# The last 512 columns of an encoder layer's second token tile: nine steps whole, seven in halves, and the mean taken off first

## The chip, the cores and the metric

One core of a Trainium2 chip. The metric is device time of one execution in microseconds (us); the kernel before takes 1071.27 us, the median of 3 runs (1070.38 to 1072.18).

## The reference

One layer of an encoder on 256 tokens of width 2048: adaLN modulation, windowed attention, LayerNorm, then a squared-ReLU MLP of width 8192 and a second LayerNorm. The change touches only the end:

```
y = sq_relu_mlp(hff, mlp_w1[i], mlp_b1[i], mlp_w2[i], mlp_b2[i])
x = layer_norm(DEEPNORM_ALPHA * x + (1.0 + g_f[:, None, :]) * y, ln_mlp_g[i], ln_mlp_b[i])

def layer_norm(x, g, b):
    mu = jnp.mean(xf, axis=-1, keepdims=True)
    var = jnp.mean(jnp.square(xf - mu), axis=-1, keepdims=True)
    y = (xf - mu) * lax.rsqrt(var + LN_EPS)
    return (y * g.astype(jnp.float32) + b.astype(jnp.float32)).astype(x.dtype)
```

## The kernel before

Tokens lie on the 128 partitions, in two tiles t = 0 and 1; the 2048 columns are four blocks c = 0 to 3 of 512. `xs` holds the residual stream, two blocks in each [128, 1024] buffer (a g in the profile), and `part(xs, t, c)` is one block of one token tile. The MLP runs in four blocks of 2048 hidden units; `us` holds the squared activations of a block, in high and low halves, and `ws` the second weight matrix, split in the same way. A product of 128 hidden units is a step of three matmuls (`mm3`, L552 to L555): high x high, high x low, low x high, each [128 x 128] x [128 x 512] in fp32r with its own weight load. Products accumulate in PSUM tiles `pa` (one bank each, five in turn).

A scheduler orders the instructions on each engine by the program's order, by priorities (`tc.high_priority`) and by what depends on what. Engines then run apart and wait on semaphores; VectorE, ScalarE and SP each take their instructions in their order.

The end of the program, from L1255 on, is the last block's c = 3. For each t, 16 steps (`ff_mm`, 48 matmuls) fill one bank. `add_gated` (L833) multiplies it by the gate g2 (L836), adds it to xs (L837) and takes bn_stats of 512 columns (L838). For t = 0 follow `norm_scalars` and two passes over each of the four blocks: minus mean, times g (L1295), then times rstd, plus b (L1296), and the store (L1280): odd c from SP's queue, even c from ScalarE's. While TensorE makes t = 1, VectorE does this; before it, `scaled` (L1284) multiplies blocks 0 to 2 of t = 1 by -0.5 g.

For t = 1 the kernel writes the normalisation as z x q + (b + nm x g), with z = -0.5 g x, q = -2 rstd and nm = 0.5 x mean x q. `last_scalars` (L1258 to L1273) makes q from a square root on ScalarE (L1263) and a Newton step on VectorE (L1265 to L1270), and nm (L1272). TensorE adds b and nm x g in PSUM for c = 1, 2, 3: an identity matmul of b ahead of time (L1304), then a matmul of g with a diagonal dg of nm, which ScalarE writes (L1309, L1317). These two are fp32 matmuls, which the profile shows as two passes each. For c = 0 VectorE makes w = g x nm + b (L1313). Block 3 is scaled by L1284 late, since its sum is just done. Four output passes z x q + (bank or w) end the program (L1318), c = 0, 1, 2, 3, each with its store.

Of the kernel before, what the change touches and what calls it, by code (L numbers as in the profile page):

```python
# [21 lines left out]
NT = S // 128  # L22
# [6 lines left out]
LN_EPS = 1e-5  # L29
# [30 lines left out]
def hybrid_kernel(ctx: ExitStack, tc: tile.TileContext, a, out: bass.AP):  # L60
    nc = tc.nc
    cst = ctx.enter_context(tc.tile_pool(name="cst", bufs=1))
    sml = ctx.enter_context(tc.tile_pool(name="sml", bufs=4))
# [5 lines left out]
    psa = ctx.enter_context(tc.tile_pool(name="psa", bufs=5, space=PSUM))  # L69
# [28 lines left out]
    ident = cst.tile([128, 128], F32, name="ident")  # L98
# [5 lines left out]
    eps = cst.tile([128, 1], F32, name="eps")  # L104
# [377 lines left out]
    for tok in LOADS.split():  # L482
        n = [int(v) for v in tok[1:].split(",")]
# [29 lines left out]
    for n, (kg, fq) in enumerate(W1A):  # L513
        left = [m.n - m.planned for m, _, _ in m_ff]
# [32 lines left out]
    acc, xts, held, xs = {}, {}, {}, [None] * 4  # L547

    def part(tiles, t, c):
        return tiles[c][:, t * 512:t * 512 + 512]  # L550

    def mm3(ps, xh, xl, wh, wl, start, stop):  # L552
        nc.tensor.matmul(ps, xh, wh, start=start, stop=False)  # L553
        nc.tensor.matmul(ps, xh, wl, start=False, stop=False)  # L554
        S.prev = nc.tensor.matmul(ps, xl, wh, start=False, stop=stop).ins  # L555
# [118 lines left out]
    for tok in STEPS.split():  # L674
        n = int(tok[1:])
# [154 lines left out]
            nc.scalar.copy(oh, po)  # L830
            return lambda: nc.vector.tensor_sub(ol, po, f32(oh))

    def add_gated(ps, t, c, gt, stats):  # L833
        tmp = sml.tile([128, 512], F32, name="tmp", tag="t2", bufs=4)
        z = part(xs, t, c)
        nc.vector.tensor_tensor(tmp, ps, gt(c), op=OP.mult)  # L836
        nc.vector.tensor_add(z, z, tmp)  # L837
        nc.vector.bn_stats(stats[t][:, c], z)  # L838
# [82 lines left out]
    for n in range(21):  # L921
# [136 lines left out]
    g2 = None  # L1058
    uacc = [g4() for _ in range(4)]
    us = []  # L1060
    opened = {}
    for n, (kg, fq) in enumerate(W1A):
# [3 lines left out]
        wh, wl = S.main()  # L1066
        for fp in range(2):
            if kg % 2 == 0:
                opened[fq, fp] = psa.tile([128, 512], F32, name="pa")
            ps = opened[fq, fp]  # L1070
            for fi in range(2):
                o = ps[:, fi * 256:fi * 256 + 256]
                for k in range(4):
                    w = (fp * 2 + fi) * 4 + k
# [12 lines left out]
            elif kg == 3:  # L1087
                nc.vector.tensor_add(av, av, ps)
                u = g4(F32R)
# [127 lines left out]
    for blk in range(BLK - 1):  # L1217
        if blk:
            us, pm = ff_mixed(blk)
# [23 lines left out]
    st = [sml.tile([128, 4, 6], F32, name=f"st{t}", bufs=2) for t in range(NT)]  # L1243
    mid = gather(pm)
    for f in mid[:2]:
        f()
# [8 lines left out]

    ws = [S.main() for _ in range(4)]

    def last_scalars(st):  # L1258

        mv = sml.tile([128, 2], F32, name="mv")  # L1260
        nc.vector.bn_aggr(mv, st)
# [3 lines left out]
        nc.vector.tensor_scalar_add(ve, mv[:, 1:2], LN_EPS)  # L1265
        r0 = sml.tile([128, 1], F32, name="r0")
        nc.vector.reciprocal(r0, sd)
        q = sml.tile([128, 1], F32, name="qq")
        nc.vector.scalar_tensor_tensor(q, r0, ve, r0, op0=OP.mult, op1=OP.mult)
        nc.vector.scalar_tensor_tensor(q, q, -3.0, r0, op0=OP.add, op1=OP.mult)  # L1270
        nm = sml.tile([128, 1], F32, name="nmr")
        nc.vector.scalar_tensor_tensor(nm, mv[:, 0:1], 0.5, q, op0=OP.mult, op1=OP.mult)  # L1272
        return q, nm  # L1273

    def affine(c):
        return (gb[n][c // 2][:, (c % 2) * 512:(c % 2) * 512 + 512] for n in range(2))

    def store(t, c, z):
        q = nc.sync if c % 2 else nc.scalar
        q.dma_start(out[t * 128:t * 128 + 128, c * 512:c * 512 + 512], z)  # L1280

    def scaled(t, c):
        z, (g, b) = part(xs, t, c), affine(c)
        nc.vector.scalar_tensor_tensor(z, z, -0.5, g, op0=OP.mult, op1=OP.mult)  # L1284

    for t in range(NT):
        ps = psa.tile([128, 512], F32, name="pa")
        for kg in range(4):
            ff_mm(ps, us, kg, t, ws[kg], kg == 0, kg == 3)
        if t == 0:  # L1290
            add_gated(ps, t, 3, g2, st)
            mv, rstd = norm_scalars(st[t])
            for c in (1, 0, 2, 3):
                z, (g, b) = part(xs, t, c), affine(c)
                nc.vector.scalar_tensor_tensor(z, z, mv[:, 0:1], g, op0=OP.subtract, op1=OP.mult)  # L1295
                nc.vector.scalar_tensor_tensor(z, z, rstd, b, op0=OP.mult, op1=OP.add)  # L1296
                store(t, c, z)
            for c in range(3):
                scaled(1, c)
    pw = {}  # L1300
    for c in (1, 2, 3):
        pw[c] = psa.tile([128, 512], F32, name="pa")
        g, b = affine(c)
        tc.keep_in_program_order(nc.tensor.matmul(pw[c], ident, b, start=True, stop=False))  # L1304
    with tc.high_priority(200):
        add_gated(ps, 1, 3, g2, st)
        rstd, nm = last_scalars(st[1])
        dg = sml.tile([128, 128], F32, name="dg", tag="t2", bufs=4)
        nc.scalar.activation(dg, ident, AF.Copy, scale=nm)  # L1309
    scaled(1, 3)  # L1310
    g, b = affine(0)
    w = sml.tile([128, 512], F32, name="w", tag="t2", bufs=4)
    nc.vector.scalar_tensor_tensor(w, g, nm, b, op0=OP.mult, op1=OP.add)  # L1313
    for c in range(4):
        z, (g, b) = part(xs, 1, c), affine(c)
        if c:
            nc.tensor.matmul(pw[c], dg, g, start=False, stop=True)  # L1317
        nc.vector.scalar_tensor_tensor(z, z, rstd, pw[c] if c else w, op0=OP.mult, op1=OP.add)  # L1318
        store(1, c, z)


# [91 lines left out]
```

## Time and profile before

| | |
|---|---|
| median of 3 runs | 1071.27 us |
| the profiled execution's own time | 1071.01 us |
| its span, first to last instruction | 1069.2 us |
| TensorE matmuls busy | 1051.6 us |
| VectorE busy | 938.8 us |
| mean granted TensorE clock | 0.999 |
| last matmul of the second tile's c = 3 starts | 1057.52 us |
| last output pass starts | 1065.07 us |

Times in the rows are us from the start of the span. A row of the timeline has the start, the duration (of the whole run of instructions where it ends in xN), the engine, the line, the operation, the names out<-in, and in brackets the idle time before it and what ended that. A row of a group of lines has the count, busy us, the mean ns of one, and the idle time before them. PE is TensorE, PEld its weight loads, DVE VectorE, ACT ScalarE; SPq and ACTq are instructions that start a DMA.

### The profile page before, as it was taken

How to read it: one execution, taken by the hardware profiler on the slowest of the kernel's cores; microseconds unless marked ns; L12 is line 12 of the kernel's file. 1: busy time of each engine (PE TensorE's matmuls, PEld its weight loads, DVE VectorE, ACT ScalarE, POOL GpSimd, SP SyncE). 2: the span in 40 equal slices, each digit the busy share in tenths (PEclk: the TensorE clock that was granted, in tenths of full speed). 3: DMA queues.
4: the chain of work that ended last, by engine and by line, in shares of the span. 5: the costliest groups of instructions: out<-in, count | busy, mean ns of one | idle time of the engine just before them, and what ended most of it. 6: DMA issues, size and time to landing. Idle time of an engine off the chain costs nothing.

```text
span 1069.2 us, 15967 instructions
## 1 busy us (share of the span) xinstructions
PE 1051.6 (98%) x6162; PEld 853.7 (80%) x6162; DVE 938.8 (88%) x1396; ACT 620.1 (58%) x978; POOL 27.5 (3%) x54
## 2 busy tenths in 40 slices
PE   8999999999999999999999999999999999999997
PEld 6677677666677799988888888788888888888885
DVE  4689999979999998987579999999899887999997
ACT  5333347776772737643367776447677536767640
POOL 1000000001000000000000000000000001000000
PEclk9999999999999999999999999999999999999999
DMA  9999997799965998698824644974564773465742
GB/s 383 424 424 425 427 427 289 284 388 337 394 252 197 349 361 303 247 333 314 296 91 186 236 180 175 388 280 155 200 235 165 281 286 138 160 232 201 264 166 78
DMA packets 43516, 292.72 MB, mean 274 GB/s; under 512 B 5152, under 2 KB 5280, under 8 KB 9648
## 3 DMA queue, kind: packets, MB, share of 16 engines
q1 hardware_dynamic: 39456, 279.85, 68.0%
q0 software_dynamic: 3232, 10.50, 3.0%
q10 hardware_dynamic: 752, 1.35, 0.4%
q8 instruction: 48, 0.79, 0.3%
q14 instruction: 28, 0.23, 0.1%
HBM read 289.57 MB, written 2.11 MB: 273 GB/s over the span
## 4 chain that ended last, share of the span: by engine, by line
PE 87%; DMA 6%; DVE 4%; ACT 1%; issue 1%; SPq 0%; ACTq 0%; DVEq 0%
PE pa L1108 16%; PE pa L553 14%; PE pa L555 14%; PE pa L554 14%; PE pa L1110 9%; DMA raw<-in_modm 4%; PE pm L361 3%; PE pa L1081 3%; PE pa L1082 3%; PE pa L1078 3%; DVE g L401 2%; PE pa L766 1%; PE pt L810 1%; PE pa L827 1%; DMA raw<-in_w 1%; PE pt L554 1%
## 5 line engine op out<-in xcount | busy, mean ns | idle before, releaser
L297 ACT CAST wh<-raw 128x1024 fp32r<-128x1024 f32 (+1 forms) x332 | 335.9, 1021 | 268.3 <-PE pa L555 150.9
L248 DVE TENSOR_TENSOR wl<-raw,wh 128x1024 fp32r<-128x1024 f32 (+1 forms) x332 | 388.0, 1183 | 61.9 <-ACT wh L297 57.3
L553 PE MATMUL pa<-wh,g 128*128 128x512 f32 x648 | 258.1, 399 | 3.6 <-ACT g L576 2.9
L554 PE MATMUL pa<-wl,g 128*128 128x512 f32 x648 | 253.4, 391 | 0.5 <-DVE wl L248 0.5
L555 PE MATMUL pa<-wh,g 128*128 128x512 f32 x648 | 252.9, 392 | 0.9 <-DVE g L578 0.9
L1108 PE MATMUL pa<-g,wh 128*128 128x512 f32 x768 | 191.5, 391 | 0.0
L1108 PEld LDWEIGHTS pa<-g,wh 128*128 128x128 f32 x768 | 140.5, 188 | 28.4 <-issue 0.8
L553 PEld LDWEIGHTS pa<-wh,g 128*128 128x128 f32 x648 | 121.6, 188 | 40.9 <-issue 6.8
L555 PEld LDWEIGHTS pa<-wh,g 128*128 128x128 f32 x648 | 121.5, 188 | 29.7 <-DVE g L578 3.0
L554 PEld LDWEIGHTS pa<-wl,g 128*128 128x128 f32 x648 | 121.8, 188 | 25.6 <-DVE wl L248 1.2
L1110 PEld LDWEIGHTS pa<-g,wl 128*128 128x128 f32 x768 | 104.8, 190 | 7.5
L1110 PE MATMUL pa<-g,wl 128*128 128x256 f32 x768 | 107.1, 282 | 0.0
L401 DVE SCALAR_TENSOR_TENSOR g<-raw,cact,g 128x1024 f32<-128x1024 f32 x66 | 84.0, 1280 | 2.7 <-DMA raw<-in_modf 1.6
L1081 PE MATMUL pa<-g,wh 128*128 128x256 f32 x256 | 72.9, 285 | 0.2 <-DVE g L1004 0.2
L1078 PE MATMUL pa<-g,wh 128*128 128x256 f32 x256 | 72.7, 285 | 0.4 <-ACT g L996 0.3
L1082 PE MATMUL pa<-g,wl 128*128 128x256 f32 x256 | 72.3, 283 | 0.0
L248 DVE TENSOR_TENSOR raw<-raw 128x1024 fp32r<-128x1024 f32 x48 | 58.4, 1222 | 0.6 <-ACT raw L297 0.6
L297 ACT CAST raw<-raw 128x1024 fp32r<-128x1024 f32 x48 | 49.8, 1044 | 4.9 <-DVE raw L259 3.6
L401 DVE SCALAR_TENSOR_TENSOR g4b<-raw,cact,g4b 128x1024 f32<-128x1024 f32 x32 | 40.2, 1283 | 13.8 <-DMA raw<-in_modgf 13.8
L1081 PEld LDWEIGHTS pa<-g,wh 128*128 128x128 f32 x256 | 49.1, 192 | 1.4 <-DVE g L1004 0.9
L1078 PEld LDWEIGHTS pa<-g,wh 128*128 128x128 f32 x256 | 49.0, 192 | 0.8 <-ACT g L996 0.8
L1082 PEld LDWEIGHTS pa<-g,wl 128*128 128x128 f32 x256 | 49.1, 192 | 0.0
(234 smaller groups left out, 1244.1 us busy)
## 6 DMA issues: line engine op xcount, KB each, us to landing
raw<-in_w1b SPq DMA_DIRECT2D x48, 1024.0 KB, 6.6
raw<-in_w SPq DMA_DIRECT2D x40, 1024.0 KB, 7.0
raw<-in_modm SPq DMA_DIRECT2D x32, 1024.0 KB, 11.4
raw<-in_modf SPq DMA_DIRECT2D x32, 1024.0 KB, 7.3
raw<-in_wqkv SPq DMA_DIRECT2D x24, 1024.0 KB, 12.5
raw<-in_w2s SPq DMA_DIRECT2D x24, 1024.0 KB, 4.8
raw<-in_modgm SPq DMA_DIRECT2D x16, 1024.0 KB, 7.2
raw<-in_wo SPq DMA_DIRECT2D x16, 1024.0 KB, 7.3
```

The source lines that it names most:

```text
L248: self.pinned(nc.vector.tensor_sub(l[:, :w], r, f32(self.hs[n])[:, :w]))
L297: self.pinned(nc.scalar.copy(h[:, :s.shape[-1]], s))
L361: i = nc.tensor.matmul(self.ps[32 * j:32 * j + 32, :w], lhsT[j] if type(lhsT) is list else lhsT, rhs[j], start=self.first, stop=stop)
L401: nc.vector.scalar_tensor_tensor(p[:, :e], s, cact[:, kt:kt + 1], p[:, :e], op0=OP.mult, op1=OP.add)
L553: nc.tensor.matmul(ps, xh, wh, start=start, stop=False)
L554: nc.tensor.matmul(ps, xh, wl, start=False, stop=False)
L555: S.prev = nc.tensor.matmul(ps, xl, wh, start=False, stop=stop).ins
L1078: x = nc.tensor.matmul(o, wh(w, 128), hh, start=new, stop=False)
L1081: nc.tensor.matmul(o, wh(w, 128), hl, start=False, stop=False)
L1082: nc.tensor.matmul(o, wl(w, 128), hh, start=False, stop=end)
L1108: nc.tensor.matmul(ps, wh(k, 128), ff_in(k), start=k == 0, stop=False)
L1110: nc.tensor.matmul(ps[:, :256], wl(k, 128), ff_in(k)[:, :256], start=False, stop=k == NK - 1)
```

## The change

Lines of the changed kernel differ from those of the one before by 1 to 16.

- The tile's 16 steps of t = 1 are now nine whole ones (LAST = 9) into one bank, seven of the left 256 columns into the same bank, and then seven of the right 256 columns into a second bank.
- `add_gated` takes a column range. It is called for the left half, for the right half of the first bank (no statistics, since the sum isn't complete), and then for the second bank, with its own bn_stats; the statistics of a tile have five groups.
- The normalisation of t = 1 is rearranged. TensorE's identity matmul puts z = -0.5 g x of blocks 1, 2, 0 into PSUM (L1326 of the changed kernel), and dm = 0.5 x mean x identity, written by VectorE straight after the aggregate (L1267), adds 0.5 x mean x g (L1333). Block 3 is done on VectorE: (z - mean) x gneg with gneg = -0.5 g (L1273, gneg made at L1305). The output passes are bank x q + b (L1334), in the order c = 3, 1, 2, 0. nm, dg and w go.
- `keep` holds `last_scalars` and the output passes in the order they are written in.

```
+LAST = 9
...
-    def add_gated(ps, t, c, gt, stats):
+    def add_gated(ps, t, c, gt, stats, cols=slice(0, 512), n=0):
         tmp = sml.tile([128, 512], F32, name="tmp", tag="t2", bufs=4)
-        z = part(xs, t, c)
-        nc.vector.tensor_tensor(tmp, ps, gt(c), op=OP.mult)
-        nc.vector.tensor_add(z, z, tmp)
-        nc.vector.bn_stats(stats[t][:, c], z)
+        z = part(xs, t, c)[:, cols]
+        nc.vector.tensor_tensor(tmp[:, cols], ps[:, cols], gt(c)[:, cols], op=OP.mult)
+        nc.vector.tensor_add(z, z, tmp[:, cols])
+        if stats:
+            nc.vector.bn_stats(stats[t][:, c + n], z)
...
+    keep = tc.keep_in_program_order
+    def last_scalars(st, g):
         mv = sml.tile([128, 2], F32, name="mv")
-        nc.vector.bn_aggr(mv, st)
+        keep(nc.vector.bn_aggr(mv, st))
+        dm = sml.tile([128, 128], F32, name="dm", tag="t2", bufs=4)
+        keep(nc.vector.tensor_scalar(dm, ident, mv[:, 0:1], 0.5, op0=OP.mult, op1=OP.mult))
         sd = sml.tile([128, 1], F32, name="sd")
-        nc.scalar.activation(sd, mv[:, 1:2], AF.Sqrt, bias=eps)
+        keep(nc.scalar.activation(sd, mv[:, 1:2], AF.Sqrt, bias=eps))
...
+        z = part(xs, 1, 3)
+        keep(nc.vector.scalar_tensor_tensor(z, z, mv[:, 0:1], g, op0=OP.subtract, op1=OP.mult))
...
-        nm = sml.tile([128, 1], F32, name="nmr")
-        nc.vector.scalar_tensor_tensor(nm, mv[:, 0:1], 0.5, q, op0=OP.mult, op1=OP.mult)
-        return q, nm
+        return q, dm
...
+    gneg = sml.tile([128, 512], F32, name="w", tag="t2", bufs=4)
+    nc.vector.tensor_scalar_mul(gneg, gb[0][1][:, 512:], -0.5)
+    ps, pr = (psa.tile([128, 512], F32, name="pa") for _ in range(2))
+    left, right = slice(0, 256), slice(256, 512)
+
+    def last(n, p, cols, start, stop):
+        s = slice((n % 2) * 256 + 128, (n % 2) * 256 + 256)
+        u, (wh, wl) = us[n // 2], ws[n // 4]
+        mm3(p[:, cols], u[:, :512][:, s], u[:, 512:][:, s], wh(n % 4)[:, cols], wl(n % 4)[:, cols], start, stop)
+
+    for n in range(LAST):
+        last(n, ps, slice(0, 512), n == 0, False)
+    for n in range(LAST, 16):
+        last(n, ps, left, False, n == 15)
+    with tc.high_priority(200):
+        add_gated(ps, 1, 3, g2, st, left)
+        add_gated(ps, 1, 3, g2, None, right)
+    for n in range(LAST, 16):
+        last(n, pr, right, n == LAST, n == 15)
     pw = {}
-    for c in (1, 2, 3):
+    for c in (1, 2, 0):
         pw[c] = psa.tile([128, 512], F32, name="pa")
-        g, b = affine(c)
-        tc.keep_in_program_order(nc.tensor.matmul(pw[c], ident, b, start=True, stop=False))
+        keep(nc.tensor.matmul(pw[c], ident, part(xs, 1, c), start=True, stop=False))
     with tc.high_priority(200):
-        add_gated(ps, 1, 3, g2, st)
-        rstd, nm = last_scalars(st[1])
-        dg = sml.tile([128, 128], F32, name="dg", tag="t2", bufs=4)
-        nc.scalar.activation(dg, ident, AF.Copy, scale=nm)
-    scaled(1, 3)
-    g, b = affine(0)
-    w = sml.tile([128, 512], F32, name="w", tag="t2", bufs=4)
-    nc.vector.scalar_tensor_tensor(w, g, nm, b, op0=OP.mult, op1=OP.add)
-    for c in range(4):
+        add_gated(pr, 1, 3, g2, st, right, 1)
+        rstd, dm = last_scalars(st[1], gneg)
+    for c in (3, 1, 2, 0):
         z, (g, b) = part(xs, 1, c), affine(c)
-        if c:
-            nc.tensor.matmul(pw[c], dg, g, start=False, stop=True)
-        nc.vector.scalar_tensor_tensor(z, z, rstd, pw[c] if c else w, op0=OP.mult, op1=OP.add)
+        if c < 3:
+            nc.tensor.matmul(pw[c], dm, g, start=False, stop=True)
+        keep(nc.vector.scalar_tensor_tensor(z, pw.get(c, z), rstd, b, op0=OP.mult, op1=OP.add))
         store(1, c, z)
```

The order on the engines differs only in this last stretch. On VectorE before, from the first tile's last output passes to the second tile's aggregate (g_2615 is block 3 of xs, pa the bank, st_9680 the statistics of t = 1):

```order
L1296 SCALAR_TENSOR_TENSOR g_2613<-g_2613,r_9923,g_9674 128x512
L1296 SCALAR_TENSOR_TENSOR g_2615<-g_2615,r_9923,g_9674 128x512
L836 TENSOR_TENSOR tmp<-pa,g4b 128x512
L837 TENSOR_TENSOR g_2615<-g_2615,tmp 128x512
L838 BN_STATS st_9680<-g_2615 128x6
L1261 BN_AGGR mv<-st_9680 128x2
```

and in the changed kernel:

```order
L1300 SCALAR_TENSOR_TENSOR g_2613<-g_2613,r_9923,g_9674 128x512
L837 TENSOR_TENSOR tmp<-pa,g4b 128x256 x2
L838 TENSOR_TENSOR g_2615<-g_2615,tmp 128x256 x2
L840 BN_STATS st_9680<-g_2615 128x6
L1300 SCALAR_TENSOR_TENSOR g_2615<-g_2615,r_9923,g_9674 128x512
L837 TENSOR_TENSOR tmp<-pa,g4b 128x256
L838 TENSOR_TENSOR g_2615<-g_2615,tmp 128x256
L840 BN_STATS st_9680<-g_2615 128x6
L1265 BN_AGGR mv<-st_9680 128x2
```

The early work on the first bank stands ahead of the first tile's fourth output pass, and that pass ahead of the last right half (the seven steps in the second bank). On VectorE from the aggregate to the end, before:

```order
L1284 SCALAR_TENSOR_TENSOR g_2615<-g_2615,g_9672 128x512
L1265 TENSOR_SCALAR ve<-mv 128x1
L1267 RECIPROCAL r_10009<-sd 128x1
L1269 SCALAR_TENSOR_TENSOR qq<-r_10009,ve 128x1
L1270 SCALAR_TENSOR_TENSOR qq<-qq,r_10009 128x1
L1272 SCALAR_TENSOR_TENSOR nmr<-mv,qq 128x1
L1313 SCALAR_TENSOR_TENSOR w<-g_9671,nmr,g_9673 128x512
L1318 SCALAR_TENSOR_TENSOR g_2609<-g_2609,qq,w 128x512
L1318 SCALAR_TENSOR_TENSOR g_2611<-g_2611,qq,pa 128x512
L1318 SCALAR_TENSOR_TENSOR g_2613<-g_2613,qq,pa 128x512
L1318 SCALAR_TENSOR_TENSOR g_2615<-g_2615,qq,pa 128x512
```

and in the changed kernel:

```order
L1267 TENSOR_SCALAR dm<-ident,mv 128x128
L1271 TENSOR_SCALAR ve<-mv 128x1
L1273 SCALAR_TENSOR_TENSOR g_2615<-g_2615,mv,w 128x512
L1275 RECIPROCAL r_10043<-sd 128x1
L1277 SCALAR_TENSOR_TENSOR qq<-r_10043,ve 128x1
L1278 SCALAR_TENSOR_TENSOR qq<-qq,r_10043 128x1
L1334 SCALAR_TENSOR_TENSOR g_2615<-g_2615,qq,g_9674 128x512
L1334 SCALAR_TENSOR_TENSOR g_2611<-pa,qq,g_9673 128x512
L1334 SCALAR_TENSOR_TENSOR g_2613<-pa,qq,g_9674 128x512
L1334 SCALAR_TENSOR_TENSOR g_2609<-pa,qq,g_9673 128x512
```

dm, on which TensorE waits, now stands first, and block 0's output, whose store goes from ScalarE's queue, last. Another row that moved: the scaling of g (w<-g_9672, L1305) stands in the changed kernel between L837 and L838 of the first tile's c = 3. On TensorE the 48 matmuls of t = 1 are followed by the identity products and those with dg or dm as before.

More of the change, by code (lines that the diff above doesn't have):

```diff
@@ L1242, in hybrid_kernel @@
             nc.gpsimd.dma_start(gb[n][h], a["lnrow"][2 + n:3 + n, h * 1024:h * 1024 + 1024].partition_broadcast(128))
-    st = [sml.tile([128, 4, 6], F32, name=f"st{t}", bufs=2) for t in range(NT)]
+    st = [sml.tile([128, 5, 6], F32, name=f"st{t}", bufs=2) for t in range(NT)]
     mid = gather(pm)
@@ L1256, in hybrid_kernel @@
     ws = [S.main() for _ in range(4)]
-    def last_scalars(st):
+    keep = tc.keep_in_program_order
+    def last_scalars(st, g):
         mv = sml.tile([128, 2], F32, name="mv")
-        nc.vector.bn_aggr(mv, st)
+        keep(nc.vector.bn_aggr(mv, st))
+        dm = sml.tile([128, 128], F32, name="dm", tag="t2", bufs=4)
+        keep(nc.vector.tensor_scalar(dm, ident, mv[:, 0:1], 0.5, op0=OP.mult, op1=OP.mult))
         sd = sml.tile([128, 1], F32, name="sd")
-        nc.scalar.activation(sd, mv[:, 1:2], AF.Sqrt, bias=eps)
+        keep(nc.scalar.activation(sd, mv[:, 1:2], AF.Sqrt, bias=eps))
         ve = sml.tile([128, 1], F32, name="ve")
-        nc.vector.tensor_scalar_add(ve, mv[:, 1:2], LN_EPS)
+        keep(nc.vector.tensor_scalar_add(ve, mv[:, 1:2], LN_EPS))
+        z = part(xs, 1, 3)
+        keep(nc.vector.scalar_tensor_tensor(z, z, mv[:, 0:1], g, op0=OP.subtract, op1=OP.mult))
         r0 = sml.tile([128, 1], F32, name="r0")
-        nc.vector.reciprocal(r0, sd)
+        keep(nc.vector.reciprocal(r0, sd))
         q = sml.tile([128, 1], F32, name="qq")
-        nc.vector.scalar_tensor_tensor(q, r0, ve, r0, op0=OP.mult, op1=OP.mult)
-        nc.vector.scalar_tensor_tensor(q, q, -3.0, r0, op0=OP.add, op1=OP.mult)
-        nm = sml.tile([128, 1], F32, name="nmr")
-        nc.vector.scalar_tensor_tensor(nm, mv[:, 0:1], 0.5, q, op0=OP.mult, op1=OP.mult)
-        return q, nm
+        keep(nc.vector.scalar_tensor_tensor(q, r0, ve, r0, op0=OP.mult, op1=OP.mult))
+        keep(nc.vector.scalar_tensor_tensor(q, q, -3.0, r0, op0=OP.add, op1=OP.mult))
+        return q, dm
     def affine(c):
@@ L1284, in scaled @@
         nc.vector.scalar_tensor_tensor(z, z, -0.5, g, op0=OP.mult, op1=OP.mult)
[L1286 to L1299, printed above, removed]
+    ps = psa.tile([128, 512], F32, name="pa")
@@ new lines, in hybrid_kernel @@
+    for kg in range(4):
+        ff_mm(ps, us, kg, 0, ws[kg], kg == 0, kg == 3)
+    add_gated(ps, 0, 3, g2, st)
+    mv, rstd = norm_scalars(st[0][:, :4])
+    for c in (1, 0, 2, 3):
+        z, (g, b) = part(xs, 0, c), affine(c)
+        nc.vector.scalar_tensor_tensor(z, z, mv[:, 0:1], g, op0=OP.subtract, op1=OP.mult)
+        nc.vector.scalar_tensor_tensor(z, z, rstd, b, op0=OP.mult, op1=OP.add)
+        store(0, c, z)
+    for c in range(3):
+        scaled(1, c)
+    gneg = sml.tile([128, 512], F32, name="w", tag="t2", bufs=4)
```

## The prediction

> **What bounds the kernel now.** The page's first part says which engine fills the span, the windows view then shows the last 22 us, which are all that the change touches.
>
> ```profile
> span 1069.2 us, 15967 instructions
> ...
> PE 1051.6 (98%) x6162; PEld 853.7 (80%) x6162; DVE 938.8 (88%) x1396; ACT 620.1 (58%) x978; POOL 27.5 (3%) x54
> ```
> ```profile
> core 0: us, PE busy (x) PEld busy (x) DVE busy (x) ACT busy (x) POOL busy (x), PEclk, DMA share, GB/s
> 1047.00:1058.00 11.00, 11.00 (x50) 9.06 (x49) 8.84 (x19) 0.20 (x1) 0.00 (x0) 1.00 0.23 88
> 1058.00:1069.20 11.20, 5.32 (x12) 1.81 (x10) 7.24 (x15) 0.69 (x2) 0.00 (x0) 0.92 0.26 101
> ```
>
> TensorE is busy 98% of the span. Up to 1058 it has no gap (11.00 of 11.00); after that comes a tail of 11.2 us in which it works 5.32 and VectorE 7.24. The profiled execution took 1071.01 us, 1.8 more than its span; the median of the runs shown is 0.26 above it. Everything before the second tile's column block c = 3 keeps its place, so the sum is over this tail. The chain that ended last gives its links:
>
> ```profile
> 1057.68 0.24 PE pa L555
> 1057.94 0.70 DVE tmp L836
> 1058.67 0.70 DVE g L837
> 1059.39 0.70 DVE st L838
> 1060.12 0.26 DVE mv L1261
> 1060.39 0.55 DVE g L1284
> 1061.10 0.23 DVE qq L1269
> 1061.74 0.41 ACT dg L1309
> 1062.19 2.86 PE pa L1317 x6
> 1065.07 0.75 DVE g L1318
> ```
>
> Three VectorE passes of 0.69 after the last product, the statistics, a scalar chain up to dg, then 2.86 us of TensorE (three fp32 products, two passes each) and the last output pass, ending at 1065.82. The remaining 3.39 us are the last store and the program's close.
>
> **Part 1, TensorE: 21 matmuls of 512 columns become 42 of 256.** From the timeline and from the line of the only short matmuls of this shape:
>
> ```profile
> 1048.00 0.39 PE L555 MATMUL pa<-wh,g 128*128 128x512 f32 x1
> ...
> 1057.52 0.39 PE L555 MATMUL pa<-g4b,g 128*128 128x512 f32 x1
> ```
> ```profile
> 1004.76 1.11 PE L1110 MATMUL pa<-g,wl 128*128 128x256 f32 x8
> ```
> ```profile
> L1110 PEld LDWEIGHTS pa<-g,wl x768: 187/192/192, 542.2 to 1005.5; 128*128 128x128 f32 x192
> L1110 PE MATMUL pa<-g,wl x768: 277/283/283, 542.4 to 1005.6; 128*128 128x256 f32 x192
> ```
>
> The first two rows are 42 steps apart (48 matmuls of the tile, five issued earlier between those of the first tile), so one 512-column matmul costs 9.52 / 42 = 0.227. Eight of 256 columns take 1.11, the last of them its own 0.28, so the step is 0.83 / 7 = 0.119; I take 0.12. The 21 that change began at 1057.52 - 20 x 0.227 = 1052.98. Now the last left matmul starts at 1052.98 + 20 x 0.12 = 1055.38 and ends 0.28 later, 1055.67; the last right one starts at 1057.90 and ends at 1058.19. So TensorE ends 0.28 later than before (1057.91), but the left half, and the right half of the first nine steps, are ready 2.2 us earlier. Bounds of the step: half of a whole one, 0.113, and the weight load's 0.192 if loads didn't overlap; I take 0.12 because the eight rows are the same shape.
>
> The Trainium skill (TensorE: Matmul & The Clock Gate, Back-to-back issue gap) tabulates 262 cycles for 256 columns and 518 for 512, at 2.4 GHz 109 and 216 ns. By that the cut would cost 21 x 2.5 ns = 0.05 us instead of 0.28, an estimate; the trace's 0.119 against 0.227 says more, and I go by the trace.
>
> **Part 2, VectorE up to the statistics.** Here lies the point: was VectorE free to use the early half? Its rows, then the groups that price the new shapes:
>
> ```profile
> 1045.70 1.89 DVE L1284 SCALAR_TENSOR_TENSOR g<-g,g 128x512 f32<-128x512 f32 x3
> 1048.20 0.69 DVE L836 TENSOR_TENSOR tmp<-pa,g4b 128x512 f32<-128x512 f32 x1 [0.61 <-PE pa L555]
> 1048.92 0.69 DVE L837 TENSOR_TENSOR g<-g,tmp 128x512 f32<-128x512 f32 x1
> ...
> 1053.83 2.74 DVE L1296 SCALAR_TENSOR_TENSOR g<-g,r,g 128x512 f32<-128x512 f32 x4
> 1057.94 0.69 DVE L836 TENSOR_TENSOR tmp<-pa,g4b 128x512 f32<-128x512 f32 x1 [1.37 <-PE pa L555]
> ```
> ```profile
> L1041 DVE TENSOR_TENSOR g<-uf,g 128x256 fp32r<-128x256 f32 x48 | 20.3, 422 | 3.7 <-ACT g L1040 3.7
> ...
> L1050 DVE TENSOR_TENSOR sf<-uf 128x128 f32<-128x128 f32 x24 | 7.0, 291 | 6.8 <-ACT uf L1038 6.8
> ...
> L577 DVE TENSOR_SCALAR g<-g,scm,shm 128x256 f32<-128x256 f32 x16 | 6.5, 408 | 1.7 <-ACT g L576 1.7
> ...
> L399 DVE TENSOR_SCALAR g<-raw,cact 128x1024 f32<-128x1024 f32 x6 | 4.5, 748 | 0.2 <-DMA raw<-in_modm 0.2
> L1002 DVE TENSOR_SCALAR g<-pt,a,b 128x256 f32<-128x256 f32 x8 | 4.2, 539 | 0.2 <-ACT g L996 0.2
> ...
> L867 DVE TENSOR_SCALAR g<-g,mv,r 128x512 f32<-128x512 f32 x4 | 2.0, 542 | 0.0
> ...
> L134 DVE TENSOR_SCALAR ang<-pack,posf 128x32 f32<-128x32 f32 x2 | 0.4, 238 | 0.0
> ```
>
> VectorE works on the first tile from 1048.20 without a pause till 1056.57 and then idles 1.37. Three L1284 of 0.685 take 1.89: an operation that needs nothing of the one before starts 0.08 before that one's end; one that does (L837 after L836) starts 0.03 after it. With that:
> - The new scaling of g by -0.5 (128x512) stands between L836 and L837 of the first tile. It lies between 0.41 (L577, half as wide) and 0.75 (L399, twice as wide); near L867's 0.542, which has two pointers where this has none, so 0.48. L837 starts 0.28 later, and so does all behind it.
> - The four L1296, 0.75 each, stand (2.74 - 0.75) / 3 = 0.664 apart, the fourth at 1055.82. In that place, 1056.11 with the delay, stand now two multiplications, two additions and one bn_stats of 256 columns. The left products are there since 1055.71, so nothing waits. Each costs 0.42 by L1041, 0.336 net of the overlap: 1056.11 + 5 x 0.336 = 1057.79. The range of one is 0.29 (L1050) to 0.69 (the whole).
> - Then the fourth output pass of the first tile, 0.664: till 1058.45. The second bank's product is ready at 1058.23, so **VectorE, not TensorE, is late now, by 0.22**.
> - Multiplication, addition, bn_stats (0.42 + 0.03 each) and the aggregate (0.26): till 1060.08. Before, 1060.38.
>
> So the split gains only 0.3 us: of the 1.37 us idle and the 3 x 0.27 us saved by halving the passes behind the last product, the scaling (0.28) and the five early pieces (1.68) take most back.
>
> The Trainium skill (VectorE: DVE Perf Modes, The TRN2 errata) speaks against the cut: a fixed cost per instruction, to be spread over tiles of 512 elements or more. Its formula for fp32 tensor_tensor, (N + 151) / 0.96, gives 424 ns at 256 as an estimate, and the rows agree (422 for 256, 686 for 512). By it the five early pieces stay as priced; what it leaves out is that they lie in VectorE's idle time.
>
> **Part 3, from the statistics to the end.**
>
> ```profile
> 1057.75 2.73 PE L1304 MATMUL pa<-g,ident 128*128 128x512 f32 x6
> ...
> 1061.55 0.16 DVE L1272 SCALAR_TENSOR_TENSOR nmr<-mv,qq 128x1 f32<-128x1 f32 x1
> 1061.74 0.40 ACT L1309 ACTIVATE dg<-ident,nmr 128x128 f32<-128x128 f32 x1 [1.02 <-DVE nmr L1272]
> 1061.74 0.75 DVE L1313 SCALAR_TENSOR_TENSOR w<-g,nmr,g 128x512 f32<-128x512 f32 x1
> 1062.19 0.30 PEld L1317 LDWEIGHTS pa<-g,dg 128*128 128x128 f32 x2 [2.54 <-ACT dg L1309]
> 1062.19 2.84 PE L1317 MATMUL pa<-g,dg 128*128 128x512 f32 x6 [1.71 <-ACT dg L1309]
> ```
>
> The diagonal needs only the mean now, so the sqrt, its Newton step, nmr, ScalarE's dg and w leave TensorE's path. dm, one pointer on 128 columns, lies between L134's 0.238 and L577's 0.408: 0.29, nearer to the first. It runs 1060.11 to 1060.40. TensorE's three identity products, 2.73 us before (L1304) and begun 0.23 after the last step's start, now occupy it till about 1060.7, so the mean's products start there rather than at 1062.19, and end at about 1061.7, 1062.6 and 1063.4.
>
> VectorE goes on with ve (0.14) and the z pass (0.75) while ScalarE's sqrt runs beside it, then the reciprocal and two steps for q (0.16 as L1272, the first of the two 0.23 as L1269, with gaps of 0.03): till 1061.64. Four output passes follow, at 0.664 steps: c = 3 at 1061.67, then c = 1, 2, 0 at 1062.34, 1063.00, 1063.66, each later than its product. The last ends at 1063.66 + 0.75 = **1064.41, against 1065.82: 1.41 earlier**. Before, the outputs were paced by TensorE at 0.86; now VectorE paces them.
>
> The last store moves from SP to ScalarE's queue, and stores come 0.66 apart instead of 0.86:
>
> ```profile
> out<-g SPq DMA_DIRECT2D x4, 256.0 KB, 2.3
> out<-g ACTq DMA_DIRECT2D x4, 256.0 KB, 2.5
> ```
>
> From issue to landing 2.3 to 2.5; the price is 0 to 0.2, and I take 0.2, as the queue is ScalarE's. **Sum: -1.41 + 0.2 = -1.2 us**: 1069.8 from the profiled execution, and 1070.1 from the median, which I forecast. That is 0.11%; a measurement of this kernel tells about 0.2% (2.14 us) from no change.
>
> **Rivals.**
> - *The cuts cost more than their rows say.* VectorE has no slack in my count from 1048.2 to the end, so every extra counts in full. If the three halves read from PSUM cost L1002's 0.539 (+0.36), bn_stats doesn't shrink (2 x 0.27), g's scaling costs 0.75 (+0.27) and dm 0.41 (+0.12), 1.29 us go: no change, 1071.4. Against it: L836 from PSUM costs what L837 from SBUF costs, 0.69. Chance 0.18, with all of it or half.
> - *VectorE is sooner free.* With 0.35 for a half it waits for TensorE at 1058.23 (-0.22), the outputs can't come before 1063.4 + 0.75, and a 2.3 landing gives -0.2 more: -1.65, 1069.6. More isn't in the tail; faster by over 0.2% comes only with the spread of the runs (1070.38 to 1072.18). Chance of over 0.2%: 0.06.
> - *Short matmuls aren't overlapped, and it is slower.* The place is the 42 matmuls. L1110's rows come eight in a row, each a product of low parts; here every third operand changes from high to low and back, as in the whole steps. If each cost its own 0.283, the last would end at 1064.87, the second bank would wait 6.45 us longer, and the time be 1070.1 + 6.45 = 1076.5, slower by 0.5%. It decides at a step of 0.207: (1061.79 - 0.32 - 1052.98) / 41. Against it: weights change in L1110 too (768 loads for 768 matmuls). Chance 0.04.
> - *It doesn't do what it says.* The built order has left, right, identity, mean, and one early bn_stats; only the fourth output pass of the first tile stands ahead of the second bank, counted above.
>
> **How the numbers follow.** Forecast 0.72 (1069.6 to 1070.8), costly cuts 0.18, over 0.2% faster 0.06, slower 0.04. The range takes in both ends of the unknown costs (1069.6 to 1071.4) and the runs' spread below: 1069.0 to 1071.5. Within 0.2%: 0.9; faster 0.06; slower 0.04.
>
> **What would show it.** Right: the last 256-column matmul starts near 1057.9; no VectorE idle between the first tile's passes and the aggregate; the fourth output pass ends near 1058.45, the aggregate near 1060.1; TensorE's mean products start by 1060.8; output passes 0.66 apart, the last near 1064.4. Wrong: a matmul step above 0.13, halves above 0.45, an output pass waiting for TensorE, or a last store landing over 2.6 us after its issue.

## The result, and the profile after

| | before | changed |
|---|---|---|
| median of 6 runs each | 1071.09 us (1070.38 to 1072.18) | 1075.32 us (1073.57 to 1076.97) |
| ratio, 95% interval | | 1.0034 [1.0024, 1.0045] |
| profiled execution, its span | 1071.01, 1069.2 us | 1076.62, 1074.8 us |

The changed kernel is 0.34% slower, where 0.11% faster was forecast. The tail does what was forecast; the loss lies ahead of it, where the order of the work is the same. The page of the changed kernel, then two windows that are cut like those of before (busy time and count of instructions for each engine, granted clock, DMA share, GB/s):

```profile
span 1074.8 us, 16013 instructions
...
PE 1057.3 (98%) x6183; PEld 857.1 (80%) x6183; DVE 939.6 (87%) x1401; ACT 620.1 (58%) x977; POOL 27.5 (3%) x54
```

```profile
core 0: us, PE busy (x) PEld busy (x) DVE busy (x) ACT busy (x) POOL busy (x), PEclk, DMA share, GB/s
1054.00:1065.00 11.00, 11.00 (x70) 9.99 (x69) 10.25 (x24) 0.20 (x1) 0.00 (x0) 1.00 0.19 72
1065.00:1074.80 9.80, 5.21 (x13) 1.98 (x11) 5.98 (x15) 0.29 (x1) 0.00 (x0) 0.87 0.37 134
```

TensorE is busy 5.7 us longer (1057.3 against 1051.6). The 21 matmuls more account for about 0.3 of it (42 short ones at 0.12 us for 21 whole ones at 0.227), and the tail after the last gap-free stretch is 9.8 us instead of 11.2. VectorE's timeline of the changed tail (start, duration, line, operation):

```profile
1055.08 0.69 DVE L837 TENSOR_TENSOR tmp<-pa,g4b 128x512 f32<-128x512 f32 x1 [0.61 <-PE pa L556]
1055.69 0.42 DVE L1305 TENSOR_SCALAR w<-g 128x512 f32<-128x512 f32 x1
...
1062.91 0.75 DVE L837 TENSOR_TENSOR tmp<-pa,g4b 128x256 f32<-128x256 f32 x2
...
1064.58 0.73 DVE L1300 SCALAR_TENSOR_TENSOR g<-g,r,g 128x512 f32<-128x512 f32 x1
1065.23 0.42 DVE L837 TENSOR_TENSOR tmp<-pa,g4b 128x256 f32<-128x256 f32 x1
...
1066.60 0.29 DVE L1265 BATCH_NORM_AGGREGATE mv<-st 128x2 f32<-128x30 f32 x1
1066.93 0.28 DVE L1267 TENSOR_SCALAR dm<-ident,mv 128x128 f32<-128x128 f32 x1
...
1068.49 0.75 DVE L1334 SCALAR_TENSOR_TENSOR g<-g,qq,g 128x512 f32<-128x512 f32 x1
1069.16 2.06 DVE L1334 SCALAR_TENSOR_TENSOR g<-pa,qq,g 128x512 f32<-128x512 f32 x3
```

and TensorE's last rows:

```profile
1064.66 0.28 PE L555 MATMUL pa<-g4b,g 128*128 128x256 f32 x1
1064.78 0.28 PE L556 MATMUL pa<-g4b,g 128*128 128x256 f32 x1
1064.90 2.74 PE L1326 MATMUL pa<-g,ident 128*128 128x512 f32 x6
1067.47 2.74 PE L1333 MATMUL pa<-g,dm 128*128 128x512 f32 x6
```

The first row of VectorE is the point that both tails share: VectorE takes up the product of the first tile, at 1048.20 before and at 1055.08 now. Counted from it (us):

| | before | forecast | changed |
|---|---|---|---|
| last matmul of the right half starts | | 9.70 | 9.70 |
| fourth output pass of the first tile ends | | 10.25 | 10.23 |
| aggregate ends | 12.19 | 11.88 | 11.81 |
| mean's products start | 13.99 | 12.5 | 12.39 |
| last output pass ends | 17.62 | 16.21 | 16.14 |
| span ends | 21.01 | 19.8 | 19.76 |

So the tail gained 1.25 us, as forecast (1.2). But it began 6.88 us later. To see where that arose, the two traces are laid beside each other at the same products, which can be done because TensorE's order is the same up to the tail (the first 6129 matmuls of the two traces agree in operands and shape). Two such products (the 4285th and the 6019th matmul of the program), first of before and then of the changed kernel:

```profile
687.12 0.39 PE L553 MATMUL pa<-wh,g 128*128 128x512 f32 x1
...
1027.82 0.39 PE L553 MATMUL pa<-wh,g 128*128 128x512 f32 x1
```

```profile
692.75 0.39 PE L554 MATMUL pa<-wh,g 128*128 128x512 f32 x1
...
1034.71 0.39 PE L554 MATMUL pa<-wh,g 128*128 128x512 f32 x1
```

The same 1734 matmuls take 340.70 us before and 341.96 after, in a stretch in which neither trace shows TensorE waiting. So the step from one matmul to the next has become longer. The whole span, cut at such products (by their number in the program), with the experiments that are told below:

| stretch, us | before | changed | wide stats | only sc | all 128 | moved back |
|---|---|---|---|---|---|---|
| start to 1531 | 222.65 | 224.11 | 223.93 | 223.30 | 224.38 | 222.58 |
| 1531 to 1939 | 67.08 | 69.70 | 67.32 | 66.82 | 68.41 | 66.83 |
| 1939 to 3571 | 258.73 | 258.75 | 258.63 | 260.21 | 258.64 | 258.49 |
| 3571 to 4251 | 130.15 | 130.83 | 130.80 | 130.82 | 130.16 | 130.17 |
| 4251 to 4285 | 8.51 | 9.36 | 9.05 | 9.02 | 9.68 | 8.81 |
| 4285 to 6019 | 340.70 | 341.96 | 341.85 | 341.85 | 340.46 | 340.49 |
| 6019 to the end | 41.39 | 40.13 | 41.82 | 41.37 | 41.38 | 40.16 |

What had changed there, if not the order? The change makes the two statistics tiles `st` one group longer, [128, 5, 6] for [128, 4, 6]: 120 bytes of a partition instead of 96. In the built programs (a profile shows no addresses) each of their four buffers takes 128 bytes where it took 96, and every buffer that is allocated behind them stands 128 bytes further on: `raw` from byte 38656 to 38784 of a partition, `wh` from 79616 to 79744, `wl`, `g` and `g4b` alike. Before, all of them began on a multiple of 256 bytes; now they begin 128 beside one. `sc` (byte 20480), which is allocated ahead of `st`, stayed. The theory to be tested is that these **places** cost the time (P in the expectations; later R, which puts it in places relative to each other). Its rivals there are G, that spells of half clock came by chance, and C, that the longer program is to blame.

### The profile page after: what moved, and what is told of

It is laid out like the page before. It is cut to its first block, busy times and chain, and to the rows that moved or that the text cites. A ratio compares the mean times of both kernels' runs of the same rounds, so it can differ in the third digit from the quotient of the medians.

```text
span 1074.8 us, 16013 instructions
## 1 busy us (share of the span) xinstructions
PE 1057.3 (98%) x6183; PEld 857.1 (80%) x6183; DVE 939.6 (87%) x1401; ACT 620.1 (58%) x977; POOL 27.5 (3%) x54
## 4 chain that ended last, share of the span: by engine, by line
PE 83%; DMA 7%; DVE 7%; ACT 1%; issue 1%; SPq 0%; DVEq 0%; ACTq 0%
PE pa L1110 16%; PE pa L554 13%; PE pa L556 13%; PE pa L555 13%; PE pa L1112 9%; PE pa L1083 3%; PE pa L1084 3%; PE pa L1080 3%; PE pm L362 3%; DMA raw<-in_modm 2%; DVE g L402 1%; DVE wl L249 1%; PE pa L767 1%; DMA raw<-in_w 1%; PE pa L828 1%; DMA g<-in_xT 1%
```

## The experiments

Each row of a median stands beside the median of the kernel before on the same chip: 1072.35 in the first four experiments, 1072.26 in the next four, 1071.96 in the last four. The ratio is not the quotient of the two medians and can differ from it by some 0.1%. "Mean step" is the mean distance from the start of a 512-column matmul to the start of the next one, between the 3571st and the 6001st product and over the distances below 260 ns, some 1650 of them: 228.51 ns before, 229.96 in the changed kernel.

### The tile alone, without the change

The kernel before, with only its statistics tile made one group wider; the fifth group isn't used.

```
-    st = [sml.tile([128, 4, 6], F32, name=f"st{t}", bufs=2) for t in range(NT)]
+    st = [sml.tile([128, 5, 6], F32, name=f"st{t}", bufs=2) for t in range(NT)]
-            mv, rstd = norm_scalars(st[t])
+            mv, rstd = norm_scalars(st[t][:, :4])
-        rstd, nm = last_scalars(st[1])
+        rstd, nm = last_scalars(st[1][:, :4])
```

> The kernel before with only the statistics tiles widened from four groups to five (the fifth unused), so that every buffer allocated behind them lies 128 bytes further on in each partition; no instruction differs. Theory P (place): the time lost before the tail comes from where the big buffers lie, so this kernel loses it without gaining the tail's 1.4 us: 1076 to 1077 us, with matmul steps of 233 to 241 ns in the mixed MLP blocks where the kernel before has 227. Theory G (gate): the half-clock spells at 48 and 291 us came by chance and have nothing to do with the kernel: 1071 us, at times 1.5 to 3 more. Theory C (code): the longer program is to blame: 1071 us always.

Measured: 1075.17 us, ratio 1.0035 [1.0022, 1.0048]. Mean step 229.97. The two products of above in this kernel:

```profile
689.73 0.39 PE L553 MATMUL pa<-wh,g 128*128 128x512 f32 x1
...
1031.58 0.39 PE L553 MATMUL pa<-wh,g 128*128 128x512 f32 x1
```

341.85 us, with the instructions of before. 24 bytes in each buffer that nobody reads cost 0.35% by the ratio (2.8 us, 0.26%, by the medians; 1076 to 1077 us were expected). The rivals G and C had 1071 us here. So the wider tile alone makes a loss. It needn't be all of it: the changed kernel, whose tail is shorter, lost 0.34% in spite of that.

### The change with its buffers moved back

```
+            sml.tile([128, 224], F32, name="pad", bufs=1)
```

The changed kernel with an unused tile of 896 bytes behind the first `st` tiles, so that everything behind `st` stands 1024 bytes further on than before, on a multiple of 256 again.

> The changed kernel with 896 unused bytes behind the first statistics tiles, so that all buffers behind lie 1024 bytes further on than in the kernel before, at the same place modulo 1024. Theory P: only the tail's gain is left, 1069.7 us (1071.1 less 1.4), all matmul steps at 227 ns. Theories G and C: 1075 us as the changed kernel.

Measured: 1070.2 us (1069.3 to 1071.9), ratio 0.9982 [0.9972, 0.9992]: faster than both kernels, and the lowest median of all that were run. G and C had 1075 us here. Mean step 228.54. Its tail on VectorE, from the first half of the second tile's block on:

```profile
1055.58 0.75 DVE L837 TENSOR_TENSOR tmp<-pa,g4b 128x256 f32<-128x256 f32 x2
...
1057.90 0.42 DVE L837 TENSOR_TENSOR tmp<-pa,g4b 128x256 f32<-128x256 f32 x1
...
1059.28 0.29 DVE L1266 BATCH_NORM_AGGREGATE mv<-st 128x2 f32<-128x30 f32 x1
...
1061.84 2.06 DVE L1335 SCALAR_TENSOR_TENSOR g<-pa,qq,g 128x512 f32<-128x512 f32 x3
```

The distances are those of the changed kernel (the second bank is taken up 2.32 behind the first in both, and 1.38 ahead of the aggregate or 1.37), but all of it 7.33 us earlier. The gain that the tail was forecast to bring is there once the buffers are back. This kernel and the changed one differ only in places, and their ratios, 1.0034 and 0.9982, lie 0.52% apart: more than the 0.35% of the wider tile alone, but with these intervals the two can't be told apart.

### How far is far: 256 and 64 bytes

The kernel before with the same unused tile, of 256 bytes and of 64.

```
+            sml.tile([128, 64], F32, name="pad", bufs=1)
```

> The kernel before with 256 unused bytes in the same place. Theory P with a grid of 256 bytes (the buffers start at multiples of 256 before, and at 128 past one after the change): 1071 us. Theory P with a coarser grid of 512 or 1024 bytes: 1074 to 1077 us. Theories G and C: 1071 us.

Measured: 1072.56 us, ratio 1.0002 [0.9993, 1.0011], mean step 228.57: no loss. Having been moved costs nothing; what counts is the place within 256 bytes.

```
+            sml.tile([128, 16], F32, name="pad", bufs=1)
```

> The kernel before with 64 unused bytes in the same place. Theory P: at least as slow as with 128 bytes, 1076 us or more, if what counts is how a row of a buffer falls on a grid of 256 bytes or less. Theories G and C: 1071 us.

Measured: 1074.31 us, ratio 1.0018 [1.0009, 1.0027]. That is a miss, as a time at least that of the wide statistics was expected, and the mean step is 228.77, almost that of before. So the loss has two parts, of which 64 bytes bring only one. The other shows in the stretch from 10 to 100 us, in which the input loads fill the DMA engines (their share is 1.01 in both). First before, then this kernel:

```profile
10.00:100.00 90.00, 85.60 (x803) 63.98 (x794) 64.82 (x97) 36.84 (x51) 1.91 (x2) 1.00 1.01 425
```

```profile
10.00:100.00 90.00, 84.26 (x799) 62.87 (x788) 64.10 (x96) 36.94 (x51) 1.91 (x2) 1.00 1.01 419
```

The last column is GB/s: 425 against 419. It is 419 in the changed kernel too, 420 with the wide statistics, 424 after a move by 256 and 425 with the buffers moved back. The loads arrive later, and the 1531st product comes at 224.26 instead of 222.65. That the loads delay it is argued from this; no run holds the loads alone back.

### Which buffer?

Unused tiles of 128 bytes between the pools put one group of buffers at a time 128 bytes beside the grid of 256 and leave the others on it. Weights alone (`wh`, `wl`, the high and low parts that are moved through TensorE); then activations alone (`g`, `g4b` and the load buffers behind them); then `raw` alone; then only the scratch and small scalars. Of the two lines the first stands ahead of the first pool to be moved, the second ahead of the next one.

```
+    ctx.enter_context(tc.tile_pool(name="pad0", bufs=1)).tile([128, 32], F32, name="pad0")
+    ctx.enter_context(tc.tile_pool(name="pad1", bufs=1)).tile([128, 32], F32, name="pad1")
```

> The kernel before with only the converted weights (wh, wl) 128 bytes off the grid. TensorE streams them in the MLP's second product and loads them as weights in its first. If its reads of them cost the extra: 1074 to 1076 us and 229.9 ns; if the cost is elsewhere: 1071 to 1072.5 us and 228.5 ns.

Measured: 1080.98 us, ratio 1.0084 [1.0067, 1.0101], mean step 232.55. The two products:

```profile
691.68 0.39 PE L555 MATMUL pa<-wh,g 128*128 128x512 f32 x1
...
1036.88 0.40 PE L555 MATMUL pa<-wh,g 128*128 128x512 f32 x1
```

345.20 us instead of 340.70: moving one side of the products costs far more than moving both, as the change did, and more than the 1074 to 1076 us that were expected.

> The kernel before with only the buffers g and g4b (activations, residual stream, gates) and the three extra early load buffers 128 bytes off the grid. If TensorE's reads of the activations cost the extra: 1074 to 1076 us and 229.9 ns; if not: 1071 to 1072.5 us and 228.5 ns. If each kind of buffer pays its own part, this and the two runs beside it each show 0.5 to 2 us.

Measured: 1080.51 us, ratio 1.0076 [1.0061, 1.0091], mean step 231.74. The other side alone costs about the same, again beyond what was expected. If a place off the grid were slow in itself, these two would cost less than the wide statistics, which move both groups and more; each costs about double. So the theory in that form falls. What fits is that **the two operands of a matmul stand differently on the grid**: `wh` and `wl` against `g` here. In the changed kernel these stand alike again, and it is the products with `sc` that are left with unlike operands.

> The kernel before with only the weight loads' buffers (raw) of the main pool 128 bytes off the 256-byte grid; all others stay on it. If the cost sits in the transfers into raw and the conversions out of it: 1074 to 1076 us, and a mean matmul step of 229.9 ns in the mixed blocks. If it sits where TensorE reads the converted weights or the activations: 1071 to 1072.5 us and 228.5 ns.

Measured: 1073.05 us, ratio 1.0007 [0.9997, 1.0016]; mean step 229.76. The time is not to be told from before, while the steps are nearly as slow as with the wide statistics. That is no contradiction: in the stretches of the fourth and sixth rows of the table this trace is 1.4 us longer than that of before, and the interval reaches to 1.7.

This kernel also speaks on the large loads of weights, which go into `raw` and, early on, into three more buffers behind `g`. First the wide statistics, then `raw` alone:

```profile
10.00:100.00 90.00, 84.63 (x804) 63.24 (x794) 64.42 (x96) 36.82 (x51) 1.91 (x2) 1.00 1.01 420
```

```profile
10.00:100.00 90.00, 86.19 (x802) 64.71 (x795) 64.72 (x96) 36.80 (x51) 1.91 (x2) 0.98 1.01 423
```

With `raw` off the grid the rate is 423 GB/s, with the activations and the three early buffers off it 423 too, and also with `sc` alone (below), into which nothing is loaded. So that the place of the loads' own targets makes them slow is not shown: 419 to 420 came only where everything behind `st` was moved, by 64 or 128. (The clock of 0.98 with `raw` alone comes from a spell of half clock; the kernel moved by 256 has one in this stretch too, at 424.)

> The kernel before with only the small scratch tiles (tmp, rl, uf, sf, w, gb and the scalars) 128 bytes off the grid. TensorE reads none of them, so a cost in its reads gives 1071 to 1072.5 us; a cost in VectorE's and ScalarE's work on them gives 1074 us or more.

Measured: 1072.21 us, ratio 0.9998 [0.9989, 1.0007]; mean step 228.52. The scratch of VectorE and ScalarE costs nothing that these runs can tell when it stands 128 bytes beside the grid.

### Alike, but off the grid; and sc alone

If unlike places are the cause, moving everything by 128 bytes, `sc` too, must give TensorE its speed back, and moving `sc` alone must cost what the change cost there. The first kernel has only the first of the two tiles; the second has both, and the second tile puts the rest back on the grid.

```
+    sml.tile([128, 32], F32, name="pad", bufs=1)
     fixed = sml.tile([128, 1024], F32, name="sc", bufs=1)
+    sml.tile([128, 32], F32, name="pad2", bufs=1)
```

> The kernel before with 128 unused bytes ahead of every buffer of the kernel's working set: sc, raw, wh, wl, g and tmp all lie 128 bytes off the 256-byte grid, alike. Theory R (relative): TensorE pays when the two buffers that it reads at once lie differently on the grid; here they don't, so 1071 to 1072.5 us and 228.5 ns a step in the mixed blocks, products with sc included. Theory A (absolute): each buffer off the grid costs by itself: 1075 us or more and 229.9 ns, as with wide statistics tiles.

Measured: 1073.96 us, ratio 1.0018 [1.0008, 1.0027]. Mean step 228.60. The two products:

```profile
691.27 0.39 PE L554 MATMUL pa<-wh,g 128*128 128x512 f32 x1
...
1031.73 0.39 PE L554 MATMUL pa<-wh,g 128*128 128x512 f32 x1
```

340.46 us: TensorE is as fast as before. The time is above the 1071 to 1072.5 us that were expected: 2.0 us of loss are left, and they come with the slower loads (420 GB/s, the 1531st product at 224.38), as after the move by 64.

> The kernel before with sc alone (the sums of activations that are the weights in half of the mixed blocks' products) 128 bytes off the grid, all else on it. Theory R: sc against wh and raw lies as in the kernel with wide statistics tiles, so the products with sc take 231 to 237 ns a step and the time is 1073 to 1075 us. Theory A: sc is one buffer of 36, 1071 to 1072.5 us.

Measured: 1075.19 us, ratio 1.0033 [1.0021, 1.0046]. Mean step 229.95, and the loads at 423 GB/s. Products of `raw` with `sc`, first in the kernel before, then here:

```profile
1006.41 0.40 PE L553 MATMUL pt<-raw,sc 128*128 128x512 f32 x1
...
1008.46 0.39 PE L553 MATMUL pa<-raw,g 128*128 128x512 f32 x1
```

```profile
1010.55 0.39 PE L555 MATMUL pt<-raw,sc 128*128 128x512 f32 x1
1010.78 0.40 PE L556 MATMUL pt<-raw,sc 128*128 128x512 f32 x1
1011.02 0.40 PE L557 MATMUL pt<-raw,sc 128*128 128x512 f32 x1
1011.26 0.40 PE L555 MATMUL pm<-raw,sc 128*128 128x512 f32 x1
...
1012.64 0.39 PE L555 MATMUL pa<-raw,g 128*128 128x512 f32 x1
```

Nine matmuls with `sc` take 2.09 us instead of 2.05 (the two steps from the second to the fourth row 0.24 each, where 0.227 is the rule). Sorted by the names of their operands, the steps below 260 ns have these means (the last row is the group of L1108 of before):

| mean step, ns | before | all 128 | sc alone | raw alone | weights alone | activations alone |
|---|---|---|---|---|---|---|
| `pa<-wh,g` | 227.6 | 227.8 | 227.8 | 227.8 | 232.5 | 232.3 |
| `pa<-wh,sc` | 227.5 | 228.1 | 235.6 | 228.6 | 235.8 | 227.9 |
| `pm<-raw,sc` | 227.6 | 227.6 | 235.8 | 232.3 | 232.3 | 227.4 |
| `pa<-g,wh` | 228.8 | 228.8 | 230.0 | 229.9 | 232.9 | 232.6 |

The first two rows are slow in just those kernels in which their own two operands stand unlike, wherever on the grid these are. But the pair is not all of it: with the weights alone moved `pm<-raw,sc` is slower, and with `sc` or `raw` alone `pa<-g,wh` is, although both of their operands stand on the grid. Why is open, and it isn't small: of the 1.8 us in the fourth and sixth rows of the table of stretches, the products with `sc` make 1.1 and those of L1108 0.9.

One buffer of 4 KB, moved by 128 bytes, makes the matmuls of the kernel as slow as the change did. Its time is 3.2 us above that of before, of which these steps explain 1.8 (the fourth and sixth rows of the table); another 1.5 lies between the 1939th and the 3571st product. With only the small scratch moved, which costs nothing, this stretch took 260.42 too, so it isn't put down to `sc`.

### The parts of the tail

Both with the buffers moved back. First the last block in 16 whole steps again, with the rearranged normalisation kept:

```
+    for n in range(16):
+        last(n, ps, slice(0, 512), n == 0, n == 15)
...
+        add_gated(ps, 1, 3, g2, st)
+        rstd, dm = last_scalars(st[1][:, :4], gneg)
```

> The changed kernel moved back by 896 bytes, with all 16 steps whole in one bank and the gated sum and statistics in one piece: the rearranged normalisation alone. The sums of the prediction give 0.3 us less gain than with the halves: from the first tile's gated product to the last output pass 16.5 us, against 17.62 before and 16.15 with the halves, and 1070.7 us. If instead the halves carry the gain, it is 17.4 us or more.

Measured: 1071.7 us, ratio 0.9998 [0.9989, 1.0007]: not to be told from before, where 1070.7 was expected. The tail tells more than the time:

```profile
1059.39 0.69 DVE L837 TENSOR_TENSOR tmp<-pa,g4b 128x512 f32<-128x512 f32 x1 [1.17 <-PE pa L556]
...
1064.10 2.06 DVE L1328 SCALAR_TENSOR_TENSOR g<-pa,qq,g 128x512 f32<-128x512 f32 x3
```

VectorE idles 1.17 us ahead of the whole product, as before (1.37), and the last pass ends 16.52 us behind the first tile's product, against 17.62 before and 16.16 with the halves. So the rearranged normalisation brings 1.10 and the halves 0.36.

Then the halves again, with the scaling of g by -0.5 on ScalarE:

```
-    nc.vector.tensor_scalar_mul(gneg, gb[0][1][:, 512:], -0.5)
+    nc.scalar.activation(gneg, gb[0][1][:, 512:], AF.Copy, scale=-0.5)
```

> The changed kernel moved back by 896 bytes, with gneg made by ScalarE, which is idle there, instead of VectorE. If VectorE is the late one behind the halves, as the prediction has it, the second bank's product is taken up 0.1 to 0.2 us earlier, as soon as TensorE has it, and the stretch from the first tile's gated product to the last output pass is 15.9 to 16.05 us against 16.15; the time 1070 us, not to be told from the kernel beside it. If TensorE is the late one, nothing changes.

Measured: 1071.01 us, ratio 0.9996 [0.9984, 1.0008], not to be told from the one with the scaling on VectorE, nor from before. So of the three kernels with the buffers moved back only the first shows the gain in its time; in the other two it rests on the traces. In the trace the second bank's product is taken up 10.02 us behind the first tile's, 0.04 after TensorE's end, where it was 10.16 with the scaling on VectorE; the last pass ends at 16.02 instead of 16.16. VectorE had been the late one, by 0.13 us.

## Why the prediction was wrong, point by point

- **The step that failed** is the sentence "Everything before the second tile's column block c = 3 keeps its place, so the sum is over this tail." What kept its place was the order of the instructions. The buffers did not: the diff's line `st = [sml.tile([128, 5, 6]...` moved them by 128 bytes. The fifth group entered the sum only as one more bn_stats. None of its rivals was about where buffers lie; its slower rival, with a chance of 0.04, gave a time near the measured one (1076.5) by a mechanism that isn't there, which is luck.
- **Part 1 was right.** The 256-column step is 0.120 (0.12 forecast). With the 0.109 that the prediction worked out, as an estimate, from the 262 cycles that the Trainium skill tabulates (TensorE: Matmul & The Clock Gate, Back-to-back issue gap) the trace doesn't agree. The slower rival's 0.283 is excluded.
- **Part 2 was right**, within 0.1 us: a half costs 0.42, the fourth output pass stands ahead of the second bank's product and VectorE is late there, by 0.13 where 0.22 was forecast. The scaling of g cost 0.42, not 0.48. The split's gain, 0.36 by the kernel with whole steps, was forecast at 0.3.
- **Part 3 was right.** dm 0.28 (0.29), the mean's products start 12.39 us behind the shared point (12.5), the output passes stand 0.66 apart, VectorE paces them, and the last is 1.48 earlier (1.41). From its end to the span's end are 3.62 us instead of 3.39: 0.23 for the last store (0.2).
- **What was missing in the sum**: the slower matmul steps, 0.68 + 1.26 = 1.9 us (fourth and sixth rows of the table), and the later start: the 1531st product comes 1.3 to 1.7 late, with slower loads, in the kernels that have no other change there (wide statistics, all 128). With the tail's -1.25 that makes +2.0 to +2.4, against +4.2 measured (interval of the ratio: +2.6 to +4.8). The rest, 0.2 to 2.8 us, isn't settled. In the profiled execution it lies between the 1531st and the 1939th product (+2.6) and between the 4251st and the 4285th (+0.9). Both stretches differ from kernel to kernel without a rule by place (66.8 to 69.7, and 8.0 to 9.8 over the kernels run), and in the first of them the execution has a spell of half clock. First the changed kernel, then before:

```profile
48.30:51.70 3.40, 3.40 (x9) 2.29 (x7) 2.06 (x3) 0.00 (x0) 0.00 (x0) 0.51 1.00 416
290.70:294.10 3.40, 3.40 (x13) 1.48 (x10) 3.40 (x6) 2.55 (x5) 0.00 (x0) 0.50 0.89 352
```

```profile
48.30:51.70 3.40, 3.40 (x43) 2.55 (x42) 3.39 (x5) 1.05 (x1) 0.00 (x0) 1.00 1.00 418
290.70:294.10 3.40, 3.40 (x20) 2.90 (x20) 3.40 (x12) 1.92 (x10) 0.00 (x0) 1.00 0.92 378
```

The column behind POOL is the granted clock: 0.5 in both windows now, 1.00 before. The kernel moved by 256 bytes, which loses nothing, has such a spell too, at 48.7 us, and the wide statistics, which lose, have none. So a spell isn't a consequence of the places; whether the change makes it more frequent can't be told from one profile of each kernel.

What is shown: the wider tile alone makes a loss of 0.35%, moving the buffers back removes the loss, and products of `wh` with `g` or `sc` are slower when the two stand 128 bytes apart on a grid of 256. Also shown is that the loads are slower when everything behind `st` is off that grid. Not shown are which buffer slows the loads, why products with like operands slow down too, and why the memory does any of this.

## What to carry to other kernels

A tile's size is part of a change even if nobody waits for the tile: list which buffers move in memory, and by how much, before you say that the rest of the kernel stays as it is. Keep the operands of TensorE alike on a grid of 256 bytes; the place that cost nothing here, for products and loads, was all of them on it. Where a small tile must grow, pad it (shown by the kernel that was moved back) or allocate it last (not tried). And where the same instructions in the same order take longer, compare the step from one to the next over a stretch without waits, before you look for a wait.

## What the runs showed of the hardware

- The mean step of `pa<-wh,g`, 512 columns, is 227.6 to 227.8 ns with both operands alike on the grid of 256 bytes, on it (before, moved by 256) or 128 beside it (all 128), and 232.3 to 232.5 with one operand 128 bytes beside the other. For `pa<-wh,sc` it is 227.5 to 228.1 alike, and 235.6 to 236.0 with 128 bytes between the two (`sc` alone, weights alone, wide statistics). Moving `wh` and `wl` alone makes the 1734 matmuls between the two products 4.5 us slower (345.20 against 340.70), 1.3%.
- Everything behind `st` moved by 64 bytes, which sets only `sc` apart from the rest, makes little difference to the steps (228.77 against 228.51), but goes with the same slower loads as a move by 128: 419 GB/s instead of 425 while the DMA engines are full, 1.4%.
- The granted clock falls to 0.5 for 3.4 us at a time, at 48 us and at 291 us in the changed kernel and not at all there in before, with the same instructions in the same order. Such a spell need not cost much: after the one at 48.7 us the kernel moved by 256 bytes reaches its 1531st product at 223.21, 0.56 later than before.
